# One transformer kernel: other stated orders at the beginning, in the feed-forward tails, around the attention block and in the PEER queries

## The chip, the cores and the metric

The kernel runs on one core of a Trainium2 chip. A core has five engines that each take their instructions in order: TensorE (PE) for matmuls, VectorE (DVE), ScalarE (ACT) and GpSimd (POOL) for elementwise work, and SyncE (SP), which issues most DMAs. The metric is device microseconds of one execution, the median of three runs.

## The reference

The input is a sequence of 256 tokens of width 1024 in float32, in two chunks of 128 tokens (chunk 0 and chunk 1). Two blocks follow each other. Cut to what matters:

```
h = h + 0.5 * swiglu(rms_norm(h, ln_ffn1), w1_gate, w1_up, w1_down)     # feed-forward 1
h = h + concat(hgrn2(...), latent_attention(...)) @ w_out               # mixer
h = h + 0.5 * swiglu(rms_norm(h, ln_ffn2), w2_gate, w2_up, w2_down)     # feed-forward 2
h = h + sigmoid(rms_norm(h, ln_ple) @ w_ple_gate) * (p @ w_ple_proj)    # per-layer gate
x = rms_norm(h, ln_final)

h1 = rms_norm(x, norm1) * (1 + sc1) + sh1                               # second block
y  = g_a * pool_mixer(h1) + g_b * forgetting_attention(q, k, v, log_f)  # 16 heads of 64
x  = x + gt1 * (y @ w_out)
h2 = rms_norm(x, norm2) * (1 + sc2) + sh2
q  = (h2 @ w_query)            # 8 heads x 2 halves x 128 = 16 query tiles of 128
sc = q . sub_keys -> top 16 of 128, twice -> top 16 of 256 candidates, softmax
x  = x + gt2 * sum over the chosen experts of gelu(h2 . expert_u) * gate * expert_v
out = rms_norm(x, final)
```

## The kernel before

Every matmul of two float32 operands is done as three products of parts: each operand is split into a high part (rounded, written by ACT, L289) and a low part (the rest, written by DVE, L290), and PE adds low x high, high x high and high x low (L319 to L321 with the tokens' tile as the stationary operand, L323 to L325 with the weights as the stationary one). Weights stream from memory in tiles of 128x1024: SP issues the DMA into `raw`, ACT and DVE split it into `wh` and `wl`, PE uses it.

The order of the work is the order of the program, changed by stated rules: `tc.issue_after(i)` puts what is written inside it behind instruction `i`, `behind_split(c)` behind the last high and low part of a normed chunk, `lag` says how many weight steps chunk 1 follows behind chunk 0, and small tables (FLAG, TLW, QORD, OUTS, YS) say which piece of work follows which. Tags and bank kinds ("mm", "sc", "pt", "acc") decide which buffer a tile gets and therefore what it waits for.

The places around the change:

- The beginning. `xload` (L268) brings `x` in four pieces on SP's queue; ACT's queue brings `col` (L272: small column constants) and two weights `w1t` in halves (L698). ACT's first activation needs `col`. The first projection works through eight weight steps for chunk 0 and, FLAG steps later, for chunk 1.
- The tails of the two feed-forward parts. The down projections of the last few tiles are put off to the end, where chunk 0 and chunk 1 each go through the pending weights; `aH`, `aL` are the parts of the last activations.
- The per-layer gate and the v projection. `ple` ends with a norm: sums of squares (L1176 to L1186), a power of -1/2 on POOL (L1196, L1199), `xs`, the scaled chunk (L458), and the scaling of the residual `xr` (L1201). `Norm.quad` (L467 to L481) transposes `xs` on PE, modulates it with `modc` on ACT and DVE, half of the columns each, into one tile `mod`, and splits that into `hH` and `hL`. The v projection (`wv`) then multiplies chunk 0 and chunk 1 with eight weights.
- The end of attention. The last heads' values, `y_tile` (L1380 to L1385, the sum of the two branches, transposed and split into `yH`, `yL`), the output projection `out_step`, `ev_out` (L1390, L1391: `gt`, and the new `xr`), the second norm (`ns` L420, `nv` L430, `ny` L431, `xs`), and the weights `qw` of the first four query tiles, which are split like all others.
- The PEER queries. `query(nt)` makes 24 matmuls with a streamed weight for nt of 4 and up and only two transposes for nt below 4, whose product has already been made in the attention block. `scores()` multiplies the query before last named with its keys (L1565) after ACT has copied it (`qT`, L1557).

## Time and profile before

| | us |
|---|---|
| median of three runs (lowest, highest) | 1575.57 (1574.95, 1575.89) |
| the profiled execution | 1574.45 |
| its span, first to last instruction | 1572.6 |
| PE busy | 1549.9 (99%) |
| DVE busy | 1125.7 (72%) |
| ACT busy | 806.6 (51%) |
| POOL busy | 83.0 (5%) |

Durations and stretches below come from the profiled execution. An engine counts as busy while it computes, not while it issues DMAs or waits on a semaphore. PE's matmuls overlap each other in its pipeline, so the time that one costs is the distance from its start to the next start, not its own duration. The idle time in brackets behind a row lies just before that instruction, on its engine; after `<-` stands what ended it.

### The profile page before, as it was taken

To read this page: it belongs to the slowest core of one execution; us is meant where nothing else is said; L and a number is where in the kernel's file an instruction comes from. 1 tells how busy PE (TensorE), PEld (TensorE's weight loads), DVE (VectorE), ACT (ScalarE), POOL (GpSimd) and SP (SyncE) were. 2 spreads that over 40 slices of the span, in tenths; PEclk is the share of its full clock that TensorE was granted. 3 is DMA by queue.
4 is the path that set the end of the run, shared out by engine and by line. 5 is a ranking of instruction groups with operands and counts; after the bars stand their busy time and mean duration, and the time that the engine had idled before them with its cause. 6 is when DMAs were issued, how large, how long until landed. Compare 5 with 4: busy or idle time off the path is not lost.

```text
span 1572.6 us, 27124 instructions
## 1 busy us (share of the span) xinstructions
PE 1549.9 (99%) x10317; PEld 1403.6 (89%) x10317; DVE 1125.7 (72%) x2206; ACT 806.6 (51%) x1533; POOL 83.0 (5%) x147
## 2 busy tenths in 40 slices
PE   9999999999999999999999999999999999999997
PEld 7999999879999879998899999999999877888886
DVE  7767768768866666557799988788986666555654
ACT  6444564554455656655554555544445445554543
POOL 1300011100000112011000000000000000000001
PEclk9999999999999999999999999999999999999999
DMA  8777754438976356442455655555446777666662
GB/s 315 242 259 255 246 170 135 140 104 298 337 227 228 123 189 200 134 135 94 150 162 186 187 175 165 162 158 161 161 158 199 248 227 232 191 190 195 215 189 87
DMA packets 84995, 299.94 MB, mean 191 GB/s; under 512 B 9632, under 2 KB 11264, under 8 KB 84608
## 3 DMA queue, kind: packets, MB, share of 16 engines
q1 hardware_dynamic: 80640, 290.86, 56.6%
q10 hardware_dynamic: 4224, 7.34, 1.4%
q8 instruction: 81, 1.33, 0.3%
q14 instruction: 50, 0.41, 0.1%
HBM read 294.95 MB, written 3.15 MB: 190 GB/s over the span
## 4 chain that ended last, share of the span: by engine, by line
PE 89%; DMA 4%; DVE 3%; ACT 2%; issue 1%; POOL 0%; ACTq 0%; POOLq 0%; DVEq 0%
PE mm L323 15%; PE mm L324 15%; PE mm L325 15%; PE acc L319 12%; PE acc L321 11%; PE acc L320 11%; DMA raw<-in_pv 2%; DMA raw<-in_wmod 2%; DVE wl L290 1%; PE acc L1673 1%; ACT wh L289 1%; PE acc L1674 1%; PE acc L925 1%; PE sc L1290 1%; PE mm L1565 0%
## 5 line engine op out<-in xcount | busy, mean ns | idle before, releaser
L289 ACT ACTIVATE wh<-raw 128x1024 fp32r<-128x1024 f32 (+3 forms) x605 | 528.3, 896 | 539.1 <-PE mm L324 251.9
L290 DVE TENSOR_TENSOR wl<-raw,wh 128x1024 fp32r<-128x1024 f32 (+3 forms) x605 | 611.2, 1027 | 264.7 <-ACT wh L289 260.0
L323 PE MATMUL mm<-hL,wh 128*128 128x256 f32 x1976 | 565.4, 286 | 0.0
L325 PE MATMUL mm<-hH,wl 128*128 128x256 f32 x1976 | 560.2, 284 | 0.0
L324 PE MATMUL mm<-hH,wh 128*128 128x256 f32 x1976 | 560.0, 283 | 0.0
L323 PEld LDWEIGHTS mm<-hL,wh 128*128 128x128 f32 x1976 | 377.6, 191 | 2.7
L324 PEld LDWEIGHTS mm<-hH,wh 128*128 128x128 f32 x1976 | 377.9, 191 | 2.0
L325 PEld LDWEIGHTS mm<-hH,wl 128*128 128x128 f32 x1976 | 377.4, 191 | 0.5
L319 PE MATMUL acc<-wh,aL 128*128 128x512 f32 x648 | 255.9, 395 | 1.6 <-DVE aL L290 1.6
L320 PE MATMUL acc<-wh,aH 128*128 128x512 f32 x648 | 253.0, 390 | 0.0
L321 PE MATMUL acc<-wl,aH 128*128 128x512 f32 x648 | 252.9, 392 | 0.0
L321 PEld LDWEIGHTS acc<-wl,aH 128*128 128x128 f32 x648 | 121.7, 188 | 28.2 <-issue 0.2
L319 PEld LDWEIGHTS acc<-wh,aL 128*128 128x128 f32 x648 | 121.9, 188 | 27.4 <-DVE aL L290 2.8
L320 PEld LDWEIGHTS acc<-wh,aH 128*128 128x128 f32 x648 | 121.8, 188 | 26.2 <-issue 0.5
L319 PE MATMUL acc<-wh,hL 128*128 128x512 f32 x224 | 89.3, 401 | 3.1 <-ACT wh L289 1.7
L320 PE MATMUL acc<-wh,hH 128*128 128x512 f32 x224 | 87.4, 392 | 0.0
L321 PE MATMUL acc<-wl,hH 128*128 128x512 f32 (+1 forms) x224 | 85.8, 391 | 0.0
L624 DVE SCALAR_TENSOR_TENSOR macc<-raw,col,macc 128x1024 f32<-128x1024 f32 x28 | 36.1, 1288 | 29.4 <-DMA raw<-in_wmod 29.3
L290 DVE TENSOR_TENSOR aL<-G,aH 128x256 fp32r<-128x256 f32 x128 | 53.6, 419 | 3.4 <-ACT aH L289 3.4
L319 PEld LDWEIGHTS acc<-wh,hL 128*128 128x128 f32 x224 | 42.5, 190 | 13.0 <-ACT wh L289 3.2
L289 ACT ACTIVATE aH<-G 128x256 fp32r<-128x256 f32 x128 | 51.2, 401 | 4.0 <-PE acc L321 4.0
L587 ACT ACTIVATE sg<-sg 128x256 f32<-128x256 f32 x36 | 14.8, 411 | 71.0 <-DVE sg L586 68.1
(469 smaller groups left out, 1620.9 us busy)
## 6 DMA issues: line engine op xcount, KB each, us to landing
raw<-in_pu SPq DMA_DIRECT2D x128, 512.0 KB, 3.5
raw<-in_pv SPq DMA_DIRECT2D x128, 512.0 KB, 4.3
raw<-in_wmod SPq DMA_DIRECT2D x48, 512.0 KB, 4.8
raw<-in_w1gu SPq DMA_DIRECT2D x36, 512.0 KB, 4.4
raw<-in_w2gu SPq DMA_DIRECT2D x36, 512.0 KB, 4.9
raw<-in_w1d SPq DMA_DIRECT2D x22, 512.0 KB, 4.8
raw<-in_w2d SPq DMA_DIRECT2D x22, 512.0 KB, 4.5
raw<-in_wout SPq DMA_DIRECT2D x16, 512.0 KB, 3.6
```

Source lines behind the costliest of these rows:

```text
L289: lasts["high"] = act.activation(H, src, AF.Copy)
L290: lasts["low"] = dve.tensor_sub(L, src, H.bitcast(F32))
L319: mm_(ps, aL, bH, start=start, stop=False)
L320: mm_(ps, aH, bH, start=False, stop=False)
L321: lasts["pe"] = mm_(ps, aH, bL, start=False, stop=stop)
L323: mm_(ps, aH, bL, start=start, stop=False)
L324: mm_(ps, aH, bH, start=False, stop=False)
L325: mm_(ps, aL, bH, start=False, stop=stop)
L624: dve.scalar_tensor_tensor(macc[j], raw, K("c", k), macc[j], op0=OP.mult, op1=OP.add)
L925: mm_(ps[:, j, c], k[pr][:, j, sl], q[pr][:, j, sl], start=True, stop=True)
L1290: mm_(ps[:, o:o + n], qa[:, hd, c * 128:c * 128 + 128], ka[:, hd, 0:n], start=True, stop=False)
L1673: mm_(ps[:, j], H[:, j], O[:, j], start=True, stop=False)
```

## The change

At the beginning `x` is loaded in pieces of other sizes, the two halves of the first weight come on ACT's queue ahead of `col`, the second weight's halves move to SP's queue, and chunk 1 follows two steps behind chunk 0 instead of four. In both tails the splits of the third and later weights stand behind the last `aH` and `aL`. In `Norm.quad` the tile `mod` is divided into two (one written by ACT, one by DVE), and the splits are made in pieces of 128x2x128. In `ple` the scaling of the residual moves from DVE to ACT, with a factor of its own (`q2`) from three small steps on POOL, and comes after chunk 1's split; the v weights get new places behind the squares, the sums, the split and the gates. At the end of attention the value bank of head 15 is of another kind, the loads of two pool weights stand behind the split, the low halves of three query weights go to GpSimd (POOL), and `ev_out(1, 1)` stands behind the low part of chunk 0. QORD, the order of the first PEER queries, interleaves the cheap and the full ones. The diff, cut to its core:

```diff
-FLAG = (4, 4)
+FLAG = (2, 4)
+TLA = (2, 2)
-QORD = [4, 5, 0, 1, 2, 3]
+QORD = [4, 0, 5, 1, 6, 2, 7, 3]
...
-    xload(0, 0)
+    xload(0, 0, 128)
     nc.sync.dma_start(cst[:, 0:128], A["cst"][:, 0:128])
-    nc.scalar.dma_start(col, A["col"])
+    xload(0, 128, 512)
...
     wraw1(0, 2, nc.scalar)
-    wraw1(1, 2, nc.scalar)
-    xload(1, 0)
+    nc.scalar.dma_start(col, A["col"])
+    wraw1(1, 2)
+    xload(1, 0, 512)
     wraw1(2)
-    xload(0, 1)
     wraw1(3)
-    xload(1, 1)
+    xload(0, 512, 1024)
+    xload(1, 512, 1024)
...
         def quads(self, c):
             for q in range(2):
                 self.quad(c, q)
+            for k in list(self.late) if c else ():
+                with self.behind_split(1), tc.high_priority(offset=-300):
+                    self.late.pop(k)()
...
-            m = self.mp.tile([128, 4, 128], F32, tag="mod", name="mod", bufs=2)
-            for i in range(4):
-                dt = 4 * q + i
-                if i < 2:
-                    act.activation(m[:, i], bk[:, i], AF.Identity, scale=self.gain(dt), bias=self.shift(dt))
-                else:
-                    dve.tensor_scalar(m[:, i], bk[:, i], self.gain(dt), self.shift(dt), op0=OP.mult, op1=OP.add)
-            self.last_hH[c] = act.activation(self.hH[:, qs, sl], m, AF.Copy)
-            self.last_hL[c] = dve.tensor_sub(self.hL[:, qs, sl], m, self.hH[:, qs, sl].bitcast(F32))
+            for u in range(2):
+                m = self.mp.tile([128, 2, 128], F32, tag="mod%d" % u, name="mod", bufs=2)
+                for i in range(2):
+                    dt = 4 * q + 2 * u + i
...
+                us = slice(4 * q + 2 * u, 4 * q + 2 * u + 2)
+                self.last_hH[c] = act.activation(self.hH[:, us, sl], m, AF.Copy)
+                self.last_hL[c] = dve.tensor_sub(self.hL[:, us, sl], m, self.hH[:, us, sl].bitcast(F32))
...
-            W = [wload(wd[f_], 1024, pw if n_ >= len(pend) - TLW[i - 1] else None) for n_, (f_, _) in enumerate(pend)]
+            W = []
+            for n_, (f_, _) in enumerate(pend):
+                with ExitStack() as order_:
+                    if n_ >= TLA[i - 1]:
+                        for a_ in last_a:
+                            order_.enter_context(tc.issue_after(ins_of(a_)))
+                    W.append(wload(wd[f_], 1024, pw if n_ >= len(pend) - TLW[i - 1] else None))
...
-                pool.tensor_scalar(v[:, 1:2], ss[:, 0:1], ss[:, 1:2], D * EPS, op0=OP.add, op1=OP.add)
-                pool.tensor_tensor(v[:, 1:2], v[:, 1:2], mhalf[:, 0:1], op=OP.pow)
-                with tc.high_priority(offset=-300), tc.issue_after(ins_of(nout.last_xs[c])):
-                    dve.tensor_scalar(xr[:, c], hg[c], v[:, 1:2], 32.0, op0=OP.mult, op1=OP.mult)
+                def late():
+                    pool.tensor_scalar(u, ss[:, 0:1], ss[:, 1:2], D * EPS, op0=OP.add, op1=OP.add)
+                    pool.tensor_tensor(u, u, mhalf[:, 0:1], op=OP.pow)
+                    pool.tensor_scalar(u, u, 32.0, None, op0=OP.mult)
+                    act.activation(xr[:, c], hg[c], AF.Copy, scale=u)
...
         def wv(kt):
-            with tc.issue_after(ins_of(nin.last_xs[0])) if kt < 5 else nin.behind_split(0):
+            with ExitStack() as order_:
+                if kt > 0:
+                    order_.enter_context(tc.issue_after(ins_of(nin.squares[0])))
+                    order_.enter_context(tc.issue_after(ins_of(nin.sums[0] if kt < 2 else nin.last_xs[0])))
+                if kt > 1:
+                    order_.enter_context(nin.behind_split(0))
+                if kt > 2:
+                    order_.enter_context(tc.issue_after(ins_of(nin.gates[1])))
                 return wload(A["wv"][kt])
...
-            po = bank("mm" if hd >= POM else "pt", (128, 2, 64))
+            po = bank("sc" if hd == 15 else "mm" if hd >= POM else "pt", (128, 2, 64))
...
-                split(raw[:, sl], H[:, sl], L[:, sl])
+                if i == 0:
+                    split(raw[:, sl], H[:, sl], L[:, sl])
+                else:
+                    act.activation(H[:, sl], raw[:, sl], AF.Copy)
+                    pool.tensor_sub(L[:, sl], raw[:, sl], H[:, sl].bitcast(F32))
...
-        with tc.issue_after(ins_of(pT_read)), tc.issue_after(ins_of(ysum)):
+        with tc.issue_after(ins_of(pT_read)):
             query_w(1)
-        with tc.issue_after(ins_of(yhigh)), tc.issue_after(ins_of(ysum)):
+        with tc.issue_after(ins_of(yhigh)):
             query_w(2)
             query_w(3)
-        ev_out(1, 1, acc[1, 1])
+        with tc.issue_after(ins_of(nout.last_hL[0])):
+            ev_out(1, 1, acc[1, 1])
```

How this moves instructions is shown at three places, engine by engine; a row is the line, the operation, what it writes and reads, and the shape. First ACT at the beginning of the program, before:

```order
L272 DMA col<-in_col 128x120
L698 DMA raw<-in_w1t 128x512 x4
L510 ACT_TABLE_LOAD
L510 ACTIVATE hH<-mm,col 128x128
L289 ACTIVATE wh<-raw 128x512 x2
L510 ACTIVATE hH<-mm,col 128x128
L289 ACTIVATE wh<-raw 128x512
L510 ACTIVATE hH<-mm,col 128x128 x2
```

and after:

```order
L713 DMA raw<-in_w1t 128x512 x2
L716 DMA col<-in_col 128x120
L518 ACT_TABLE_LOAD
L518 ACTIVATE hH<-mm,col 128x128
L290 ACTIVATE wh<-raw 128x512 x3
L518 ACTIVATE hH<-mm,col 128x128
L290 ACTIVATE wh<-raw 128x512
L518 ACTIVATE hH<-mm,col 128x128
```

`col` stood first on ACT's queue and stands third now, behind the halves of the first weight; four halves (two weights) are two.

Second GpSimd (POOL) at the end of attention, where `ns` and `ny` are small steps of the second norm (8227, 8244 and the powers 8253, 8270 for chunk 0, the others for chunk 1) and `qw11`, `qw21`, `qw31` the low parts of three query weights; before:

```order
L1351 TENSOR_TENSOR ga_6230<-ga_6230,y_8007 128x256
L420 TENSOR_SCALAR ns_8227<-ns_8227 128x1
L431 TENSOR_TENSOR ny_8253<-nv_8252,mhalf_92 128x1
L420 TENSOR_SCALAR ns_8274<-ns_8274 128x1
L431 TENSOR_TENSOR ny_8377<-nv_8376,mhalf_92 128x1
L311 CAST wh_8507<-hL_6222 128x1
```

and after:

```order
L1382 TENSOR_TENSOR ga_6233<-ga_6233,y_8024 128x256
L1497 TENSOR_TENSOR qw11_8358<-raw_8359,qw10_8357 128x512 x2
L1497 TENSOR_TENSOR qw21_8366<-raw_8367,qw20_8365 128x512 x2
L1497 TENSOR_TENSOR qw31_8374<-raw_8375,qw30_8373 128x512 x2
L421 TENSOR_SCALAR ns_8244<-ns_8244 128x1
L421 TENSOR_SCALAR ns_8291<-ns_8291 128x1
L432 TENSOR_TENSOR ny_8270<-nv_8269,mhalf_92 128x1
L432 TENSOR_TENSOR ny_8400<-nv_8399,mhalf_92 128x1
L312 CAST wh_8536<-hL_6225 128x1
```

Six low halves now stand ahead of the norm's steps, and chunk 0's power (`ny`) stands behind chunk 1's `ns`.

Third ACT at the first PEER queries, where `wh` is the high part of a streamed query weight, `qT` the copy of a query and `G` that of its scores; before:

```order
L289 ACTIVATE wh_8699<-raw_8697 128x1024
L1557 ACTIVATE qT_8536<-mm_8504 128x256
L289 ACTIVATE wh_8750<-raw_8748 128x1024
L1557 ACTIVATE qT_8570<-mm_8538 128x256
L1567 ACTIVATE G_8478<-mm_8572 128x256
L1557 ACTIVATE qT_8593<-mm_8590 128x256
L1567 ACTIVATE G_8478<-mm_8595 128x256
L1557 ACTIVATE qT_8609<-mm_8606 128x256
L1567 ACTIVATE G_8478<-mm_8611 128x256
```

and after:

```order
L290 ACTIVATE wh_8715<-raw_8713 128x1024
L1593 ACTIVATE qT_8565<-mm_8533 128x256
L1593 ACTIVATE qT_8570<-mm_8567 128x256
L1603 ACTIVATE G_8507<-mm_8572 128x256
L290 ACTIVATE wh_8779<-raw_8777 128x1024
L1593 ACTIVATE qT_8622<-mm_8590 128x256
L1603 ACTIVATE G_8507<-mm_8624 128x256
L1593 ACTIVATE qT_8638<-mm_8635 128x256
L1603 ACTIVATE G_8507<-mm_8640 128x256
L290 ACTIVATE wh_8823<-raw_8821 128x1024
L1593 ACTIVATE qT_8683<-mm_8651 128x256
```

Before, two weight splits come with the first two copies and then none until the transposed queries are through; now a split precedes every second copy.

## Rows read from the trace of the kernel before

**Rows 1.** what PE waited for over the whole run: us in total, times, longest

```profile
PE acc L319 <- DVE hL L481: 4.3, 3, 1.7
```

**Rows 2.** windows: length, then busy us of PE, PEld, DVE, ACT, POOL; PEclk; DMA

```profile
5.00:16.00 11.00, 9.61 (x46) 6.59 (x45) 7.14 (x13) 7.89 (x16) 0.49 (x1) 1.00 1.03 397
505.00:530.00 25.00, 25.00 (x126) 20.86 (x125) 16.10 (x31) 13.00 (x30) 0.92 (x3) 1.00 0.73 246
550.00:560.00 10.00, 8.02 (x37) 6.43 (x36) 9.88 (x22) 4.82 (x11) 0.20 (x1) 0.83 0.57 211
560.00:570.00 10.00, 8.61 (x42) 6.61 (x41) 6.54 (x15) 4.37 (x13) 3.78 (x6) 1.00 0.26 79
725.00:765.00 40.00, 35.00 (x181) 28.18 (x181) 28.26 (x63) 21.67 (x50) 2.35 (x7) 1.00 0.39 139
765.00:800.00 35.00, 34.37 (x290) 34.02 (x290) 30.42 (x144) 17.68 (x35) 0.00 (x0) 1.00 0.46 145
```

**Rows 3.** timeline of ACT, beginning: start, us, instruction, [idle before <-releaser]

```profile
4.33 1.28 ACT L510 ACT_TABLE_LOAD   x1 [4.33 <-DVE col L715]
...
7.49 0.63 ACT L289 ACTIVATE wh<-raw 128x512 fp32r<-128x512 f32 x1 [0.65 <-DMA raw<-in_w1t]
```

**Rows 4.** timeline of PE, beginning

```profile
6.89 0.50 PE L319 MATMUL acc<-wh,hL 128*128 128x512 f32 x1 [0.17 <-ACT wh L289]
...
16.02 0.48 PE L319 MATMUL acc<-wh,hL 128*128 128x512 f32 x1
```

**Rows 5.** DMA issues of the beginning: count, KB each, median us to landing

```profile
col<-in_col ACTq DMA_DIRECT2D x1, 60.0 KB, 3.3
```

**Rows 6.** timeline of DVE, between norm and modulation of block 2

```profile
547.03 4.90 DVE L290 TENSOR_TENSOR wl<-raw,wh 128x512 fp32r<-128x512 f32 x8
...
553.71 0.16 DVE L644 TENSOR_TENSOR modc<-fill,col 128x8 f32<-128x8 f32 x1
```

**Rows 7.** timeline of PE, v projection, chunk 1

```profile
564.72 1.09 PE L472 MATMUL mm<-cst,xs 128*128 128x128 f32 x8
...
568.49 0.50 PE L319 MATMUL acc<-wh,hL 128*128 128x512 f32 x1 [1.28 <-DVE hL L481]
```

**Rows 8.** timeline of DVE, end of attention

```profile
737.22 2.49 DVE L290 TENSOR_TENSOR qw<-raw,qw 128x512 fp32r<-128x512 f32 x4
...
739.63 1.29 DVE L1390 TENSOR_TENSOR gt<-acc,gt 128x512 f32<-128x512 f32 x2
...
744.53 0.89 DVE L458 TENSOR_SCALAR xs<-xr,ny 128x512 f32<-128x512 f32 x2 [0.69 <-POOL ny L431]
```

**Rows 9.** timeline of PE, starts of the two chunks' queries

```profile
749.30 0.50 PE L319 MATMUL acc<-qw,hL 128*128 128x512 f32 x1 [1.71 <-DVE hL L481]
...
757.36 0.51 PE L319 MATMUL acc<-qw,hL 128*128 128x512 f32 x1 [1.35 <-DVE hL L481]
```

**Rows 10.** GpSimd: lines L1351, L1820 (ns min/median/max) and its timeline

```profile
L1351 POOL TENSOR_TENSOR ga<-ga,y x8: 736/739/1118, 608.9 to 718.6; 128x256 f32<-128x256 f32 x8
...
L1820 POOL TENSOR_TENSOR G<-G x2: 1297/1301/1305, 1558.3 to 1560.8; 128x512 f32<-128x512 f32 x2
...
49.91 1.70 POOL L664 TENSOR_SCALAR n<-n 128x256 f32<-128x256 f32 x1
```

**Rows 11.** timelines of ACT (two rows) and PE, first PEER queries

```profile
768.87 1.06 ACT L289 ACTIVATE wh<-raw 128x1024 fp32r<-128x1024 f32 x1 [1.31 <-PE mm L324]
...
769.84 0.36 ACT L1557 ACTIVATE qT<-mm 128x256 f32<-128x256 f32 x1
...
769.24 0.38 PE L1553 MATMUL mm<-cst,G 128*128 128x128 f32 x2
...
770.25 0.71 PE L1565 MATMUL mm<-keys,qT 128*128 128x128 f32 x4 [0.64 <-ACT qT L1557]
...
770.80 0.38 PE L1553 MATMUL mm<-cst,G 128*128 128x128 f32 x2
...
771.02 0.61 PE L1565 MATMUL mm<-keys,qT 128*128 128x128 f32 x4
```

More of the change, by code (lines that the diff above doesn't have):

```diff
@@ L266, in _build, with xload @@
     xv = A["x"].rearrange("(c p) d -> p c d", p=128)
-    def xload(c, j):
-        nc.sync.dma_start(xr[:, c, j * 512:j * 512 + 512], xv[:, c, j * 512:j * 512 + 512])
-    xload(0, 0)
+    def xload(c, a, b):
+        nc.sync.dma_start(xr[:, c, a:b], xv[:, c, a:b])
+    xload(0, 0, 128)
     nc.sync.dma_start(cst[:, 0:128], A["cst"][:, 0:128])
-    nc.scalar.dma_start(col, A["col"])
+    xload(0, 128, 512)
     def C(name, a=0, n=None):
@@ L444, in __init__ @@
             self.s, self.xs, self.last_xs, self.mp = {}, {}, {}, nxp
-            self.last_hH, self.last_hL = {}, {}
+            self.last_hH, self.last_hL, self.late = {}, {}, {}
         def part(self, c, j):
@@ L592, in ffn @@
                 split(a, aH, aL)
+                last_a = lasts["high"], lasts["low"]
                 pend.append((f, (aH, aL)))
@@ L1157, in ple @@
             st, hg = {}, {}
+            squares, sums = nout.squares, nout.sums = {}, {}
+            nout.gates = {}
             gf = p1.tile([128, D], F32, name="gf")
@@ L1166, in ev @@
                 with nout.behind_split(0) if c else nullcontext():
-                    act.activation(t, ps, AF.Tanh, scale=nin.half[c])
+                    nout.gates[c] = act.activation(t, ps, AF.Tanh, scale=nin.half[c])
                     dve.scalar_tensor_tensor(t, t, 1.0, proj[:, c, sl], op0=OP.add, op1=OP.mult)
@@ L1184, in ev @@
                 else:
-                    act.activation(sq[:, 0:256], g[:, 0:256], AF.Square, accum_out=ss[:, 3:4])
+                    squares[c] = act.activation(sq[:, 0:256], g[:, 0:256], AF.Square, accum_out=ss[:, 3:4])
                     dve.scalar_tensor_tensor(sq[:, 256:], g[:, 256:], 1.0, g[:, 256:], op0=OP.mult, op1=OP.mult,
@@ L1193, in after @@
                 ss = st[c]
-                v = nrm.tile([128, 2], F32, tag="q1", name="q1")
-                dve.tensor_scalar(v[:, 0:1], ss[:, 3:4], ss[:, 4:5], ss[:, 5:6], op0=OP.add, op1=OP.add)
+                v = nrm.tile([128, 1], F32, tag="q1", name="q1")
+                sums[c] = dve.tensor_scalar(v[:, 0:1], ss[:, 3:4], ss[:, 4:5], ss[:, 5:6], op0=OP.add, op1=OP.add)
                 pool.tensor_tensor(v[:, 0:1], v[:, 0:1], mhalf[:, 0:1], op=OP.pow)
                 nout.chunk(c, hg[c], v[:, 0:1])
-                pool.tensor_scalar(v[:, 1:2], ss[:, 0:1], ss[:, 1:2], D * EPS, op0=OP.add, op1=OP.add)
-                pool.tensor_tensor(v[:, 1:2], v[:, 1:2], mhalf[:, 0:1], op=OP.pow)
-                with tc.high_priority(offset=-300), tc.issue_after(ins_of(nout.last_xs[c])):
-                    dve.tensor_scalar(xr[:, c], hg[c], v[:, 1:2], 32.0, op0=OP.mult, op1=OP.mult)
+                u = nrm.tile([128, 1], F32, tag="q2", name="q2")
+                def late():
[3 more added lines that the diff above has]
+                    act.activation(xr[:, c], hg[c], AF.Copy, scale=u)
+                nout.late[c] = late
             wl_ = [lambda k=k: wload(A["wpg"][k], 1024, pw if k >= 8 - PLW else None) for k in range(8)]
@@ L1325, in pool_group @@
             wp = sm.tile([128, 256], F32, tag="wp", name="wp")
-            nc.scalar.dma_start(wp, A["wpool"][:, g * 256:(g + 1) * 256])
+            with nin.behind_split(1) if g < 2 else nullcontext():
+                nc.scalar.dma_start(wp, A["wpool"][:, g * 256:(g + 1) * 256])
             psc = sm.tile([128, 256], F32, tag="psc", name="psc")
```

8 lines of the change are left out of this document (7 added, 1 removed).

## The prediction

> **What bounds the kernel now.** The page's engine table (shown above with the times) comes first: the reader sees there that PE is busy 99% of the span, so a step pays only where PE stands idle. The list of PE's waits comes next. Its largest entry is the wait for `hL` of a norm (L481, 4.3 us over three waits) [rows 1]. Then I set windows around each place that the change touches, and the reader compares PE's busy time with the length of each window [rows 2]. Idle time is 11.00 - 9.61 = 1.39 us at the beginning, nothing in 505 to 530 (the second feed-forward tail; the first looks the same), 1.98 + 1.39 = 3.37 us in 550 to 570 (the v projection), 5.00 us in 725 to 765 (the end of attention), and 0.63 us in 765 to 800 (the PEER queries). So no more than about 10.4 us can be won in all, and a PE delay at 775 goes through to the end, for PE has next to no idle time behind it that could swallow one. Timelines of single engines in those windows give the terms below.
>
> **The beginning.** Before, `col` is the first transfer on ACT's queue. ACT's table load waits 4.33 us for the scaled `col`; the second half of the first weight then waits 0.65 us for its DMA and comes only at 7.49 [rows 3]. PE's first matmul is at 6.89, and chunk 1 starts at 16.02 [rows 4]. After, `col` (60 KB, 3.3 us from issue to landing [rows 5]) stands behind two transfers of 256 KB. What these 512 KB cost I bound from both sides: if the queue never filled, `col` would be later by its later issue alone, about 1 us, and land at about 5; if it waited for both, it would land where the second half weight now lands, about 7.4 [rows 3]. I take 5.3, nearer to the first, because the many small pieces of `col` no longer go ahead of the large ones. The table load, the first high half and the first matmul are then about 0.7 us later (7.6). But the weights of the first two steps are there by that time, and with chunk 1 only two steps behind (FLAG 2) PE has more to do. If then no wait for weights is left, 1.39 us of idle time go and 0.7 is paid by the later start; with 0.1 for stalls of single matmuls that go too, that is a gain of 0.8 us. Ends: a gain of 1.6 (all of it, `col` in time) and a loss of 0.4 (`col` at 7.4; the start is then 2.7 later, against which stand at most 2.3 us of waits for weights and for chunk 1's turn).
>
> **The v projection.** Before, DVE does eight `wl` halves (4.90 us), the scaling of the residual and two more halves between `xs` and `modc` at 553.71 [rows 6]. PE waits for that, and the mean granted clock of 550 to 560 is 0.83 [rows 2]: after those idle microseconds and matmuls of one column it falls from its upper level (2.4 GHz) to the lower (1.2) for a while. After, `modc`, the modulation and `hL` follow `xs` at once, so chunk 0's projection starts some 2.3 us earlier. It doesn't end earlier: chunk 1's transposes start at 564.72 [rows 7] because its own norm ends there, and that chain is hardly shorter. ACT issues four DMAs back to back and splits three weights before the squares of chunk 1, and on GpSimd two small steps for the new `q2` stand ahead of the power that `xs` needs. So PE's idle time moves from 552-554 to about 561-564.7. What is won lies behind it: with `hL` in pieces of 128x256 instead of 128x512, PE can start chunk 1 after the first piece, about 567.8 instead of 568.49 [rows 7]: 0.7 us. If the idle microseconds there bring the lower clock, as those before did, transposes and two weight steps at half the pace eat it: -0.1. I take a gain of 0.3, between the two. Ends: 1.8 gain (chunk 1's norm earlier by most of chunk 0's 2.3) and 0.8 loss (its chain late by one more weight).
>
> **The end of attention.** Before, four low halves of query weights (2.49 us on DVE) stand between the last `yL` and `gt` at 739.63; `xs` follows at 744.53 [rows 8]. PE starts chunk 0's queries at 749.30 after 1.71 us of waiting and chunk 1's at 757.36 after 1.35 [rows 9]. After, six low halves are on GpSimd. DVE now has `yL` of tile 7 behind four weight halves and waits for `yL` of tile 6 first, so the outputs of chunk 0 end 0.7 us later on PE; `gt` can still start at about 738.9. `xs` needs the power step on GpSimd, which stands behind the low halves and behind the sum of chunk 1's squares; PE has only the 24 output matmuls of chunk 1 to fill the time. A low half (two inputs, 128x512) has near rows: 1.30 us for the same shape and form (L1820), 0.74 us in the median and 1.12 at most for 256 columns (L1351); the dearest is 1.70 for 256 columns, at 49.91 [rows 10]. So the bounds are 1.30 and 3.4 us (twice 1.70), and I take 1.6, near the row of the same shape and stretched a little for a busy DVE. The last four halves start once ACT has their first high half, about 736.7; they end at 743.1, before the sum of chunk 1's squares (about 743.8), which the power must follow anyway. The power then ends at about 744.6, as now, and `xs` is at most 0.2 later. The smaller pieces shorten the way from transposes to the first `hL` by a good microsecond, so chunk 0 starts at about 748.3 (1.0 earlier) and chunk 1, whose output follows `hL` at once, at about 755.9 (1.4 earlier, which takes the first in). I take 1.4. Ends: 3.0 gain (three fifths of the 5.00 idle) and 4.5 loss (rival 2). Each low half over 1.6 us shifts the chain by four times the excess.
>
> The Trainium skill, GPSIMD Engine Reference, section 1 (Specifications), says that GpSimd's way into SBUF is shared with VectorE and contends with VectorE instructions that read two SBUF inputs, as `wl` and `xr` do. The longest and the median of L1351, 1.118 / 0.739 = 1.5 [rows 10], fit that. An estimate by it would be 1.30 x 1.5 = 1.95 us for a low half and the chain 1.4 us later; by it the gain of this part is gone and the time 1577.1 us, inside the likeliest case's own range.
>
> **The queries.** The order 4,5,0,1,2,3 becomes 4,0,5,1,6,2,7,3. Queries 4 and up are 24 matmuls with a streamed weight; 0 to 3 are two transposes. The scores of a query come one query later. Before, only query 5's scores follow their own 24 matmuls with little between. The rows show what that costs: ACT first splits the next weight, whose buffer those matmuls just freed (768.87, 1.06 us), then copies `qT` (769.84, 0.36). PE starts its two transposes at 769.24; such a pair takes 0.22 (770.80 to 771.02), so from 769.46 to 770.25 it does nothing: 0.79 us [rows 11]. After, four queries (4 to 7) have only transposes and a cheap query's scores between their matmuls and their own scores, and in ACT's order the weight split stands ahead of `qT` each time. Queries 5, 6 and 7 cost 0.79 each; query 4 has no cheap scores before it, which take about 0.45 (770.25 to 770.80 less the start-up): 1.24. Together 3.6 us; gone are the 0.79 and some 0.2 of small gaps between the cheap ones. Cost: 2.6 us, all of it on PE. Ends: 0 (ACT gets `qT` out first) and 3.6.
>
> **Feed-forward tails.** The window is full [rows 2], so there is nothing to gain: 0. The splits of the third and later tail weights now wait behind the last `aH`/`aL`; PE meanwhile works on the first two weights of both chunks. If that cover were too short, one split (1.06 us on ACT, as in [rows 11]) would show. Ends: 0 and a loss of 1.1.
>
> **Sum.** -0.8 - 0.3 - 1.4 + 2.6 + 0 = +0.1 us. The profiled execution took 1574.45 us (span 1572.6 and 1.85 around it); the median of the runs, 1575.57, stands 1.12 above it. 1574.45 + 0.1 + 1.12 gives 1575.7 us. What a measurement can tell from no change is about 0.2%, or 3.15 us.
>
> **Rivals.** (1) Faster: the query order costs nothing, because `qT` leaves ACT before the weight split is due, and the end of attention gives its upper 3.0: -0.8 - 0.3 - 3.0 + 0 = -4.1, so 1571.5 us. For it: ACT is busy only 17.68 of 35 us in 765 to 800 [rows 2]. Against: where it matters the rows have the split first, then `qT` [rows 11]. (2) Slower: GpSimd's queue decides. At 3.4 us for a low half, four of them end at 750.3, and the power of chunk 0's norm, with it `xs`, the transposes and `hL`, comes 5.8 us later than now. PE can fill some of it with output matmuls that it now does earlier; chunk 0's queries start at about 754, 4.5 us late. Sum: -0.8 - 0.3 + 4.5 + 2.6 = +6.0, so 1581.6 us. It eats into the gain from 1.6 us per half on and makes the whole slower by 0.2% from about 2.7. For it: 1.70 us at 49.91; against: 1.30 for the very form [rows 10]. (3) The beginning loses: `col` lands at 7.4, +0.4 instead of -0.8, 1576.9 us. (4) In the v projection the change does nothing but move the idle time, and the lower clock with it: +0.1 instead of -0.3, 1576.1 us.
>
> **Chances.** My forecast with (3) and (4), within 0.2%: 0.54. Rival (1), and other sums of upper ends that pass 3.15 us: 0.25 faster. Rival (2), and sums of lower ends: 0.21 slower. The range from 1571.0 to 1579.5 takes in rival (1) and a low half of up to about 2.7 us; of (2) the dear end is left out. The likeliest case by itself lies between 1573.3 and 1577.6.
>
> **What would show it.** In the profile after: the table load before 5.8 us and chunk 1's first matmul before 15.5; the v projection's first matmul near 553.7, a wait of PE near 561 to 564.7, chunk 1 near 567.8; low halves on POOL of 1.3 to 1.6 us, with `ny` right behind a sum of squares and not behind a low half; four waits of PE for `qT` of 0.8 to 1.2 us between query matmuls. Wrong would be: no such waits (rival 1), POOL halves above 2.5 us with `ny` behind them (rival 2), or a gap that opens in a tail.

## The result, and the profile after

| kernel | median | lowest to highest (executions) | ratio to before, 95% interval | profiled span |
|---|---|---|---|---|
| before | 1575.57 us | 1574.06 to 1575.89 (5) | | 1572.6 us |
| changed | 1584.98 us | 1581.58 to 1586.58 (5) | 1.006 [1.0046, 1.0073] | 1584.7 us |

The change is slower by 9.4 us; the forecast was 1575.7, in a range up to 1579.5. The profiled execution of the changed kernel (1586.58) is 12.1 us longer than that of before; it is the slowest of its five, so the stretches below add up to more than 9.4. I compare the starts of TensorE's matmuls, number by number ("matmul 200" is the 200th), in the two traces; where the difference grows, time is lost:

| stretch | forecast | measured in the profiled pair |
|---|---|---|
| beginning (to matmul 200, 40 us) | -0.8 | +3.3 |
| both feed-forwards, steadily (the second with its tail) | none | +0.6 and +0.9 |
| first feed-forward tail, with the block behind it | 0 | +1.7 |
| v projection | -0.3 | 0.0 |
| end of attention (to chunk 1's queries) | -1.4 | +1.7 |
| queries | +2.6 | +3.0 |
| last stage (waits at 1293 and 1317) | none | +1.2 |

The list of PE's waits in the changed kernel (total, count, longest in us) answers to [rows 1]:

```profile
PE mm L476 <- DVE xs L459: 3.7, 1, 3.7
PE acc L320 <- ACT wh L290: 3.4, 3, 1.6
PE mm L1601 <- ACT qT L1593: 3.0, 4, 1.1
PE acc L320 <- DVE yL L1416: 2.4, 1, 2.4
...
PE acc L320 <- DVE hL L489: 1.8, 2, 0.9
PE mm L514 <- DMA xr<-in_x: 1.1, 1, 1.1
```

The wait for `hL`, largest before, fell from 4.3 to 1.8 us; those for `xs`, `wh`, `qT`, `yL` and x are new or longer. The windows of the same places (columns as in [rows 2], shifted by the delay up to there) give the sizes:

```profile
5.00:16.00 11.00, 8.27 (x30) 6.40 (x29) 6.47 (x12) 6.87 (x12) 0.96 (x1) 0.69 1.01 392
511.00:536.00 25.00, 25.00 (x124) 20.30 (x123) 20.45 (x36) 14.84 (x31) 0.00 (x0) 1.00 0.83 279
556.00:566.00 10.00, 10.00 (x54) 8.55 (x53) 9.53 (x22) 9.15 (x23) 0.77 (x1) 1.00 0.33 107
566.00:576.00 10.00, 6.32 (x26) 5.01 (x25) 6.12 (x17) 4.97 (x14) 4.08 (x6) 0.83 0.32 109
731.00:771.00 40.00, 35.26 (x168) 27.47 (x168) 27.09 (x63) 21.07 (x52) 10.23 (x13) 0.96 0.35 123
771.00:806.00 35.00, 32.01 (x264) 31.01 (x263) 29.97 (x145) 16.29 (x33) 0.00 (x0) 1.00 0.45 145
```

**Beginning.** PE is busy 8.27 of 11 us, before 9.61 [rows 2], and at a mean clock of 0.69. Timelines of PE and ACT, then two DMA issues (count, KB each, us to landing), against [rows 3 to 5]:

```profile
6.29 0.55 PE L514 MATMUL mm<-cst,xr 128*128 128x128 f32 x3 [1.15 <-DMA xr<-in_x]
...
8.96 0.80 PE L320 MATMUL acc<-wh,hL 128*128 128x512 f32 x1 [1.58 <-ACT wh L290]
9.55 0.63 PE L321 MATMUL acc<-wh,hH 128*128 128x512 f32 x1
9.98 0.63 PE L320 MATMUL acc<-wh,hL 128*128 128x512 f32 x1
...
6.73 1.28 ACT L518 ACT_TABLE_LOAD   x1 [6.73 <-DVE col L731]
8.02 0.37 ACT L518 ACTIVATE hH<-mm,col 128x128 fp32r<-128x128 f32 x1
...
xr<-in_x SPq DMA_DIRECT2D x1, 192.0 KB, 4.6
...
col<-in_col ACTq DMA_DIRECT2D x1, 60.0 KB, 4.8
```

Two transfers are late: x's second piece lets the transposes go on only at 6.29, `col` lets the table load start only at 6.73. The table load comes last of the two: it ends at 8.01, and the first high half (`hH`) begins at 8.02. The first projection matmul starts at 8.96, 2.07 later than before; the waits that go behind it give back 1.4 (e4 below starts as late, and is 0.6 behind at matmul 100). Then the matmuls stand 0.43 us apart instead of 0.23: the granted clock is at its lower level (1.2 GHz) up to 15.1 us, and that is the larger loss, about 2 us. The rest, 0.6, is a wait at 35 us.

**Queries.** Four waits, as forecast; the first, then one of the three that are alike:

```profile
775.48 0.71 PE L1601 MATMUL mm<-keys,qT 128*128 128x128 f32 x4 [1.08 <-ACT qT L1593]
...
780.36 0.71 PE L1601 MATMUL mm<-keys,qT 128*128 128x128 f32 x4 [0.64 <-ACT qT L1593]
...
774.10 1.06 ACT L290 ACTIVATE wh<-raw 128x1024 fp32r<-128x1024 f32 x1 [1.66 <-PE mm L325]
775.06 0.64 ACT L1593 ACTIVATE qT<-mm 128x256 f32<-128x256 f32 x2
```

ACT splits the next weight (774.10) and only then copies `qT` (775.06), the order of [rows 11]. Measured from start to start against the usual spacing of such matmuls, the waits are 1.24 and three times 0.80 us, 3.64 in all against 3.6 in the forecast. Only 0.6 of the 1.0 us that I took off again is gone, so the stretch costs 3.0.

**v projection.** Chunk 0 starts at 560.34 and chunk 1's transposes at 571.07 after 3.68 us of waiting, 6.6 and 6.4 us behind the forecast places (553.7 and 564.7), as everything is by then. Idle time has moved (3.68 us from 556 to 576; before 3.37 from 550 to 570), and the lower clock with it (0.57 from 571 to 575).

**End of attention.** GpSimd, DVE and PE, against [rows 8, 9]:

```profile
743.32 5.57 POOL L1497 TENSOR_TENSOR qw<-raw,qw 128x512 fp32r<-128x512 f32 x4 [4.10 <-ACT qw L1496]
...
753.19 0.57 POOL L432 TENSOR_TENSOR ny<-nv,mhalf 128x1 f32<-128x1 f32 x1
...
740.47 0.42 DVE L1416 TENSOR_TENSOR yL<-mm,yH 128x256 fp32r<-128x256 f32 x1 [2.97 <-ACT yH L1415]
...
741.66 3.57 DVE L291 TENSOR_TENSOR wl<-raw,wh 128x512 fp32r<-128x512 f32 x4
745.15 0.41 DVE L1416 TENSOR_TENSOR yL<-mm,yH 128x256 fp32r<-128x256 f32 x1
...
748.03 1.40 DVE L1422 TENSOR_TENSOR xr<-gt,xr 128x512 f32<-128x512 f32 x1
...
745.62 0.80 PE L320 MATMUL acc<-wh,yL 128*128 128x512 f32 x1 [2.40 <-DVE yL L1416]
746.21 0.63 PE L321 MATMUL acc<-wh,yH 128*128 128x512 f32 x1
```

The power `ny` stands 4.3 us behind the end of the last low half: GpSimd's queue doesn't decide. Late is `yL` of tile 7, behind that of tile 6 and four splits. One of the splits took 1.76 us instead of 0.69, and one `xr` 1.40, both beside low halves: each ended 0.55 us after the low half that was running when it began (ends at 744.68 and 748.88). PE waits 2.40 us and then runs eight matmuls at the lower clock, most of them 0.63 us long, which costs 1.7 us more (745.62 to 749.34 for nine spacings of 0.23).

The wait doesn't always bring the lower clock. e6, e10 and e16 below have the same code here; PE waits as long in them, and the clock stays up. PE of e16:

```profile
740.87 0.50 PE L320 MATMUL acc<-wh,yL 128*128 128x512 f32 x1 [2.38 <-DVE yL L1416]
741.21 0.40 PE L321 MATMUL acc<-wh,yH 128*128 128x512 f32 x1
```

In these three traces the end of attention is 0.2 us longer than before, in the changed kernel's 1.7; 1.5 of that is the clock.

### The profile page after: what moved, and what is told of

Read it like the earlier page. It is cut to its first block, busy times and chain, and to the rows that moved or that the text cites. A ratio compares the mean times of both kernels' runs of the same rounds, so it can differ in the third digit from the quotient of the medians.

```text
span 1584.7 us, 27141 instructions
## 1 busy us (share of the span) xinstructions
PE 1556.2 (98%) x10317; PEld 1405.7 (89%) x10317; DVE 1123.7 (71%) x2206; ACT 809.4 (51%) x1545; POOL 95.5 (6%) x155
## 4 chain that ended last, share of the span: by engine, by line
PE 84%; DMA 7%; DVE 4%; ACT 3%; issue 2%; POOL 0%; ACTq 0%; POOLq 0%; DVEq 0%
PE mm L324 14%; PE mm L325 14%; PE mm L326 14%; PE acc L320 11%; PE acc L322 11%; PE acc L321 11%; DMA raw<-in_wmod 3%; DVE wl L291 2%; DMA raw<-in_pv 2%; ACT wh L290 1%; PE acc L1709 1%; PE acc L1710 1%; PE acc L941 1%; PE sc L1320 1%; PE mm L1601 1%
## 5 line engine op out<-in xcount | busy, mean ns | idle before, releaser
L320 PE MATMUL acc<-wh,hL 128*128 128x512 f32 (+1 forms) x224 | 89.6, 403 | 1.8 <-ACT wh L290 1.8
L321 PE MATMUL acc<-wh,hH 128*128 128x512 f32 (+1 forms) x224 | 88.2, 396 | 0.0
```

What stands on the lines that cost most here:

```text
L320: mm_(ps, aL, bH, start=start, stop=False)
L321: mm_(ps, aH, bH, start=False, stop=False)
```

## Experiments

Times are medians with the ratio to before on the same chip. A "wait" is PE's start-to-start excess over the usual spacing. Single executions of one kernel with the new beginning lie 3 to 8 us apart (e4: 1580.47 to 1588.50), so each reading rests on a median together with a trace.

**The beginning.** e1: the old transfers and lag.

```
-FLAG = (2, 4)                      +FLAG = (4, 4)
-xload(0, 0, 128) ... xload(0, 128, 512)
+xload(0, 0) ... nc.scalar.dma_start(col, A["col"])
-wraw1(1, 2)                        +wraw1(1, 2, nc.scalar)
...
```

> The changed kernel with the old beginning (the order and pieces of the first transfers, and FLAG 4). Theory 'col': in the trace after, col lands at 6.44 instead of 4.04 us, the first projection matmul starts at 8.96 instead of 6.89, and PE's clock is at its lower level from 8.28 to 15.10; by the 200th matmul that is 3.25 us behind. So about 3.2 us come back: some 1581.8 us, 6.2 above the kernel before, matmul 200 again near 40.1 us and no low clock before 16 us. Rival 'elsewhere': the beginning only shifts work, and what is lost by 40 us returns later in the first feed-forward: within 1 us of 1585.

1581.10 us, 1.0031 [1.002, 1.0042]: 3.9 us less than the changed kernel. Matmul 200 starts 3.0 earlier, as 'col' said (3.2), and the wait in the first tail is gone too. Is it `col`? e6 puts only that back:

```
 xload(0, 128, 512)
+nc.scalar.dma_start(col, A["col"])
 wraw1(0, 2, nc.scalar)
-nc.scalar.dma_start(col, A["col"])
```

> The changed kernel with one transfer put back: the columns of constants (60 KB) are issued on ACT's queue ahead of the first weights, as before; x stays cut at 128 columns, the second weight tile stays on SP's queue, and the first projection's lag stays 2. Theory 'col': col lands near 4.0 us instead of 6.44, the table load and the first hH follow at 4.4 and 5.7 as before, and the first projection matmul starts at about 7 instead of 8.96; matmul 200 starts near 41 instead of 43.4, the time falls by 2 to 3 us to about 1582.5. Rival 'the other transfers': x or the weights land late because of what goes ahead of them on SP's queue; the first projection matmul still starts past 8.5, and the time stays at 1584 to 1585.

1583.03 us, 1.0046 [1.0031, 1.0061]. PE and ACT of that run:

```profile
7.03 0.90 PE L515 MATMUL mm<-cst,xr 128*128 128x128 f32 x3 [1.75 <-DMA xr<-in_x]
...
8.90 0.80 PE L321 MATMUL acc<-wh,hL 128*128 128x512 f32 x1
...
3.27 1.28 ACT L519 ACT_TABLE_LOAD   x1 [3.27 <-DVE col L731]
7.96 0.37 ACT L519 ACTIVATE hH<-mm,col 128x128 fp32r<-128x128 f32 x1 [3.41 <-PE mm L515]
```

The table load is early (3.27), yet the first matmul starts at 8.90 as in the changed kernel: it now waits for x's second piece (7.03). The rival holds for the start. e10 puts `col` and an uncut x first:

```
-xload(0, 0, 128)                   +xload(0, 0, 512)
-xload(0, 128, 512)                 +nc.scalar.dma_start(col, A["col"])
...
```

> The changed kernel with x's first 512 columns in one transfer again, issued first, and col first on ACT's queue; the second weight tile stays on SP's queue, the order of the rest of x and the lag of 2 stay. With col alone put back, x's second piece landed at 7.03 us and the first projection matmul stayed at 8.90. Theory 'x and col, either of which is late': now the transposes run at 4.9 us, the first hH is done before 6.5, the first projection matmul starts at about 7, TensorE keeps its upper clock, matmul 200 starts near 40.5 and the time falls by 3 us to about 1582. Rival 'the weight on SP's queue': the second weight tile is late behind x, PE waits for it after the first step, and matmul 200 starts past 41.5.

1581.51 us, 1.0037 [1.0025, 1.0049]. PE:

```profile
6.68 0.50 PE L320 MATMUL acc<-wh,hL 128*128 128x512 f32 x1 [0.68 <-ACT wh L290]
```

The first matmul starts at 6.68, the clock stays at 1.00, and matmul 100 is 0.6 us ahead of before. So x's second piece alone can hold the start (e6), and with both transfers early it is gone; `col` late alone was not run. But PE waits 5.15 us in the first tail (below) in this profiled execution, the slowest of six. e16 changes the lag alone:

```
-FLAG = (2, 4)
+FLAG = (4, 4)
```

> The changed kernel with chunk 1's first projection again four steps behind chunk 0's (FLAG 4 in place of 2); all transfers as in the changed kernel. Theory 'transfers': x's second piece and col still land past 6 us, the first projection starts near 8.9, matmul 200 at 41 to 43.5; the weight stream stays 2 to 4 us further behind than PE at the 56th weight; the time is that of the changed kernel, 1585. Rival 'lag': the four steps let weights be used up as they come, the stream's lead is back (under 1.5 us lost at the 56th weight), the first tail has no wait, and the time falls to about 1582.5.

1582.11 us, 1.0046 [1.0033, 1.006], as the rival 'lag' has it: the first matmul still starts late (8.54), but the clock stays up in this trace, the weight stream is not behind any more and the first tail has no wait.

**The first tail.** e3 takes the rule for the tail's weights out:

```
-TLA = (2, 2)
+TLA = (99, 99)
```

> The changed kernel without the rule that the splits of the third and later tail weights stand behind the last aH and aL, in both tails. Theory 'tail': PE's wait of 1.75 us at 192.69 goes, since the tail weights are split before the last activation again; 1.6 us come back, some 1583.4 us, and PE is busy through 185 to 200. Rival 'mixer weights': the wait comes from the weights of the mixer that stand in the same queue, and it stays or moves to the second tail: less than 0.5 us.

1585.46 us, 1.0054 [1.004, 1.0067]; the wait stays (1.66 us from start to start). The rule isn't its cause. In the changed kernel and in e10 it is, on PE:

```profile
194.67 0.50 PE L320 MATMUL acc<-wh,aL 128*128 128x512 f32 x1 [1.59 <-ACT wh L290]
```

```profile
194.72 0.79 PE L320 MATMUL acc<-wh,aL 128*128 128x512 f32 x1 [4.99 <-ACT wh L290]
```

PE waits for weights that ACT has not split yet. e13 and e14 go on from there: before with the rule, and e10 without it.

```
e13: before, +TLA = (2, 2)
e14: as e10, -TLA = (2, 2)  +TLA = (99, 99)
```

> The kernel before with one part of the change: in both feed-forward tails the splits of the third and later down weights wait for the last aH and aL. Theory 'lead': this order costs only where the weight stream reaches the tail late; with the old beginning it arrives early, PE does not wait at 190, and the time stays within 0.5 us of before, 1575 to 1576. Rival 'order by itself': the four weights hold their load buffers until the last a, the mixer's weights come late behind them, and PE waits 1 to 2 us at about 190; 1576.5 to 1577.5.

1577.03 us, 1.0014 [1.0005, 1.0023]. No wait in the first tail; PE is even 0.6 us earlier behind it. But two more splits then stand between `xs` and `modc` in the old v projection's order. DVE, then PE:

```profile
548.72 6.10 DVE L291 TENSOR_TENSOR wl<-raw,wh 128x512 fp32r<-128x512 f32 x10
...
557.70 0.50 PE L320 MATMUL acc<-wh,hL 128*128 128x512 f32 x1 [3.99 <-DVE hL L482]
```

Ten `wl` halves where [rows 6] has eight, and PE waits 2.15 us longer than in the wait of 1.84 that before has there. Neither theory had that place; the rival's time (1576.5 to 1577.5) came out for another reason.

> The changed kernel with x and col early again (as in the run before it, where PE then waited 5.15 us in the first tail) and without the rule for the tail's weights. Theory 'lead and order together': with the weights split as soon as they land, the wait in the first tail falls under 1.7 us, and the time by about 2 us to 1579.5. Rival 'lead alone': the stream is late in any order, the wait in the tail stays above 3 us, and the time at 1581.5.

1583.37 us, 1.0056 [1.0042, 1.007]: the wait in the tail is gone in its trace, but the median is above e10's. Inconclusive, because its weight stream was not late in that execution. What goes with the wait is this: by how much the 57th weight split on ACT (153.0 us in before) came later than before, less PE's own delay there, against the wait in the first tail:

| kernel | e16 | e13 | e14 | e1 | e2 | e7 | e3 | e9 | e6 | changed | e4 | e10 |
|---|---|---|---|---|---|---|---|---|---|---|---|---|
| stream behind PE, us | -2.5 | -2.0 | 1.3 | 1.4 | 1.4 | 2.1 | 2.7 | 2.8 | 3.4 | 3.8 | 3.8 | 5.5 |
| wait in the tail, us | 0 | 0 | 0 | 0 | 0 | 0.8 | 1.7 | 0.6 | 2.0 | 1.8 | 2.1 | 5.1 |

So the wait goes with a weight stream that has lost its lead since the beginning. It opens from about 2 us on, and its size differs from one execution to the next. The lag decides more than the transfers: in the nine traces with the lag of 2 the stream is 1.3 to 5.5 us behind, and seven of them have the wait; in the eight with the lag of 4 it is between 2.7 ahead and 1.8 behind, and none has it.

**The place in SBUF.** The changed kernel and the first four experiments all show the steady loss in the feed-forwards. e5 is before, with a tile made wider and no instruction changed:

```
-v = nrm.tile([128, 2], F32, tag="q1", name="q1")
+v = nrm.tile([128, 16], F32, tag="q1", name="q1")
```

> The kernel before with one number changed: the two small scaling tiles are 64 bytes wide instead of 8, so that every tile that stands behind them in SBUF lies 64 bytes further, as in the changed kernel; no instruction is added, removed or moved. In the changed kernel, and in all four experiments so far, the down matmuls of both feed-forwards (512 columns, the a halves as weights) stand 233 ns apart in place of 227 ns, about 0.55 us in each of the two stages. Theory 'place in SBUF': the spacing is 233 ns here too, and the span grows by 1.1 us, to about 1573.7, the time to about 1576.7. Rival 'order': the spacing comes from the neighbours in time, so it stays at 227 ns and the time at 1575.6.

1577.33 us, 1.0011 [1.0002, 1.002]. PE of before, of e5, the same down matmuls:

```profile
72.19 0.39 PE L319 MATMUL acc<-wh,tL 128*128 128x512 f32 x1
72.42 0.39 PE L320 MATMUL acc<-wh,tH 128*128 128x512 f32 x1
72.64 0.39 PE L321 MATMUL acc<-wl,tH 128*128 128x512 f32 x1
72.87 0.39 PE L319 MATMUL acc<-wh,tL 128*128 128x512 f32 x1
73.10 0.39 PE L320 MATMUL acc<-wh,tH 128*128 128x512 f32 x1
```

```profile
72.28 0.40 PE L319 MATMUL acc<-wh,tL 128*128 128x512 f32 x1
72.52 0.39 PE L320 MATMUL acc<-wh,tH 128*128 128x512 f32 x1
72.75 0.40 PE L321 MATMUL acc<-wl,tH 128*128 128x512 f32 x1
72.98 0.39 PE L319 MATMUL acc<-wh,tL 128*128 128x512 f32 x1
73.21 0.40 PE L320 MATMUL acc<-wh,tH 128*128 128x512 f32 x1
```

Five starts span 0.91 us before and 0.93 here. Over the 490 or so spacings of this kind in the two feed-forwards the mean goes from 229 to 234 ns. 'Place in SBUF' holds: 64 bytes that a new small tile (`q2`) takes shift the tiles behind it. The size came out above my 1.1: in e5's trace PE loses 1.05 us in each feed-forward, tail included, 2.1 in all, as in the median. Of the 1.7 us that the table above gives to the first tail, some 0.4 are of this kind.

**The queries.** e2:

```
-QORD = [4, 0, 5, 1, 6, 2, 7, 3]
+QORD = [4, 5, 0, 1, 2, 3]
```

> The changed kernel with the old order of the PEER queries. Theory 'lag of one': the four waits of PE for qT (1.24, 0.80, 0.80, 0.80 us) become one of 0.8; 2.6 us come back, some 1582.4 us. Rival 'hidden': the sorting on DVE after the queries sets the pace, and the waits only stand in its place: less than 0.7 us come back.

1579.84 us, 1.0027 [1.0018, 1.0036]. One of the four waits is left (0.80), and PE is 3.0 us earlier behind them; that trace has no waits in the first tail and at 1293 either, which the order of the queries doesn't reach, so the rest of the 5.1 us that its median is lower can't be put down to the order. The term holds.

**The end of attention.** e4: low halves back on DVE.

```
-if i == 0: split(...)
-else: act.activation(H...); pool.tensor_sub(L...)
+split(raw[:, sl], H[:, sl], L[:, sl])
```

> The changed kernel with the low halves of the three query weights on DVE again; all other orders at the end of attention as in the changed kernel. Theory 'shared way': beside GpSimd's low halves two DVE operations with two inputs took 1.76 (wl at 743.47) and 1.40 us (xr at 748.03) instead of 0.69; with the halves on DVE these are 0.69 again, and 1.5 to 2 us come back (1583.3). Rival 'order': what holds DVE is that yL of tile 7 stands behind yL of tile 6 and four weight halves; with six low halves more on DVE (0.60 each) nothing comes back or up to 2 us are added (1585 to 1587), and PE's wait before the output matmuls of tile 7 (2.56 us at 742.83) is as long or longer.

1580.92 us, 1.004 [1.0025, 1.0056]. DVE, then PE:

```profile
738.90 2.49 DVE L291 TENSOR_TENSOR wl<-raw,wh 128x512 fp32r<-128x512 f32 x4
...
741.78 0.50 PE L320 MATMUL acc<-wh,yL 128*128 128x512 f32 x1 [1.30 <-DVE yL L1416]
742.12 0.39 PE L321 MATMUL acc<-wh,yH 128*128 128x512 f32 x1
```

The four splits take 2.49 instead of 3.57 us, PE's wait is 1.1 shorter, and a 0.78 wait for `xs` shows instead. The clock doesn't fall, so the end of attention is 2.0 us shorter and no longer than before. But against e6, e10 and e16, where the clock doesn't fall either and the low halves are on GpSimd, it is only 0.5 us shorter: that much of the 2.0 is shown to be the low halves' price, and the 1.5 to 2 us of 'shared way' is not. The Trainium skill, GPSIMD Engine Reference, section 1 (Specifications), has GpSimd's way into SBUF shared with VectorE. The trace agrees, but the price fell on the two-input work of DVE (0.69 to 1.76 us) and less on the low half (1.30, at most 1.73 here and 1.83 in e9).

Why is there a wait at all? e7 puts two waits for `ysum` back as well:

```
as e4, and
+with ..., tc.issue_after(ins_of(ysum)): query_w(1)
+with ..., tc.issue_after(ins_of(ysum)): query_w(2) ...
```

> The changed kernel with two parts of the attention block's end put back: the queries' low halves on VectorE, and the second and third query weights held until ysum. With the low halves alone put back, PE still waited 1.47 us for yL of tile 7 and 0.78 us for xs. Theory 'VectorE's order': the weights' splits that were let ahead of yL cost that wait; without them it falls under 0.8 us, and with the smaller pieces of the last Norm the attention end is then about 1 us shorter than before, the time about 1580. Rival 'ysum was no brake': the wait stays at 1.4 to 1.5 us and the time at 1580.9, that of the low halves alone.

1584.35 us, 1.0059 [1.0046, 1.0072]; the wait is 2.69, longer. My theory falls: the low halves that e4 lets go early fill DVE while it waits for tile 6; held for `ysum` they stand ahead of `yL` of tile 7. e9 tries the bank:

```
-po = bank("sc" if hd == 15 else "mm" if hd >= POM else "pt", (128, 2, 64))
+po = bank("mm" if hd >= POM else "pt", (128, 2, 64))
```

> The changed kernel with one part put back: head 15's products go into a bank of kind mm again, not sc. In the changed kernel TensorE's order has the transposes of tile 6 only behind five steps of the output projection, 2.25 us ahead of those of tile 7 (before: 5.65 us), and PE waits 2.56 us for yL of tile 7. Theory 'bank': with the old bank the transposes of tile 6 are back between heads 14 and 15, and the wait for yL of tile 7 falls to 0.7 to 1.0 us; the time falls by 1.6 us, to about 1583.4. Rival 'low halves': the wait comes from VectorE's two-input instructions, one stretched to 1.76 us by GpSimd's low halves; it stays above 2 us, and the time at 1585.

1584.57 us, 1.0059 [1.0046, 1.0072]. PE:

```profile
750.98 1.11 PE L476 MATMUL mm<-cst,xs 128*128 128x128 f32 x8 [1.82 <-DVE xs L459]
```

The wait for `yL` is gone, and PE waits 1.82 for `xs` instead. The end of attention is 2.2 us shorter in the trace; the clock stays up there, and against e6, e10 and e16 it is 0.7 shorter. The median shows none of it, which the spread of that kernel's five runs (1581.07 to 1586.71) can hide. So e15 does the bank alone, on before. TensorE's order then differs in one thing:

```
-MATMUL mm<-cst,gb 128x128 x2
-MATMUL mm<-v_6229,pT 128x64   (six of head 15)
+MATMUL sc<-v_6229,pT 128x64   (the same six)
 ... five steps of the output projection
+MATMUL mm<-cst,gb 128x128 x2
```

> The kernel before with one part of the change: head 15's products in a bank of kind sc. This alone moves the transposes of tile 6 in TensorE's order from between heads 14 and 15 to behind five steps of the output projection. Theory 'bank': yL of tile 6 is then late on VectorE, the splits behind it too, and PE waits 2 to 2.7 us for yL of tile 7 (before 0.75); chunk 0's queries start some 1.5 to 2 us later, and the time is about 1577.2. Rival 'only with the rest': VectorE has cover for it, the wait stays under 1.2 us, the time at 1575.5.

1578.25 us, 1.0017 [1.0008, 1.0026]: slower by the bank alone. PE:

```profile
739.40 0.51 PE L319 MATMUL acc<-wh,yL 128*128 128x512 f32 x1 [2.52 <-DVE yL L1385]
```

The wait is 2.69 (before 0.75), and chunk 0's queries start 2.7 us later; 1.9 of that is the wait, and the clock falls here too (from 740.9 to 744.3). 'Bank' is shown for the wait, by taking the bank out (e9) and by putting it in (e15).

**What is worth keeping.** e8 keeps the v projection's order and the two-piece quads; e11 is before with the quads alone; e12 adds to e11 the freed query weights and the later last output.

```
e11: -m = ...tile([128, 4, 128]...)
     +for u in range(2): m = ...tile([128, 2, 128]...)
e12: as e11, -tc.issue_after(ins_of(ysum)) (twice)
     +with tc.issue_after(ins_of(nout.last_hL[0])): ev_out(1, 1, ...)
e8:  the changed kernel with all else put back, u in pool p
```

> The changed kernel with every part put back but the v projection's order and the smaller pieces of the Norm (two tiles of 128x2x128 in place of one of 128x4x128), and with the second scaling tile in a pool that opens later, so that the feed-forwards' tiles lie where they lay before. Theory: the beginning, the tails and the queries are as before, the down matmuls are 227 ns apart, the waits for the query weights' first tile are 1.0 and 1.1 us instead of 1.88 and 1.51, and the v projection comes out even: about 1.3 us faster than before, 1574.2. Rival 'the v projection loses': its early start is given back with up to 1 us more, and the time is that of before, 1575.5, or more.

> The kernel before with one part of the change: the Norm's quads in two pieces of 128x2x128 instead of one of 128x4x128. Theory: the first hL piece is ready sooner, so PE's waits ahead of chunk 0's and chunk 1's queries (1.88 and 1.51 us of excess) fall to about 1.6 and 1.1, and that ahead of chunk 1 in the v projection (1.45) falls by some 0.5; about 1.2 us faster, 1574.2. Rival: the twice as many small instructions on ACT and VectorE eat it; the waits stay, the time is 1575.3 or more.

> The kernel before with the two-piece quads and two further parts of the change: the second and third query weights no longer wait for ysum, and chunk 1's last output waits for the first hL of chunk 0. Theory: to the gain of the two-piece quads comes that chunk 1's output no longer stands between modulation and hL on VectorE, so PE's wait ahead of chunk 0's queries falls from about 1.6 to 1.0 us; 1573.5. Rival: the weights' splits that are let go earlier push yL of tile 7 back, PE waits 0.7 us more there, and the time is that of the two-piece quads alone or above it.

e8: 1574.02 us, 0.9997 [0.9989, 1.0006]; e11: 1574.77, 0.9997 [0.9988, 1.0005]; e12: 1575.51, 0.9997 [0.9988, 1.0006]. The quads do what was expected of them: waits ahead of the queries of 1.60 and 1.10 us or less in all three (1.88 and 1.51 before). But the gain of 0.7 us can't be told from no change, and in e12 PE waits 1.41 for `xs` (0.78 before), so that nothing is left. No version beats the kernel before beyond what can be measured. In e8 the feed-forwards run at the spacing of before again.

## Why the prediction was wrong

- **Beginning, -0.8: wrong, the first step that failed.** `col` landed at 6.44, inside my bounds of 5 and 7.4 but above the 5.3 I took. The table load came at 6.73 and not before 5.8. I had bounded `col` alone and never priced the cut of x, whose second piece landed at 6.24 as the third transfer of SP's queue; e6 shows that this alone can keep the start at 8.9. The start came 2.07 late, not 0.7; the waits that go gave back 1.4, as I had it. Above all I had no term for the clock here, though I had one in the v projection: e4 started at 8.91 with the same waits, its clock stayed up, and at matmul 200 it was 2.7 us ahead of the changed kernel (2.1 the clock, 0.6 the wait at 35 us). My bound of a loss of 0.4 counted a late start against waits that go, both at full clock.
- **Tails, 0: wrong.** A gap opened in a tail, the sign that I had named, and it is larger than my end of 1.1 us. I looked for cover in the tail itself. What goes with the wait is the lead that the weight stream has by then, and the new lag takes it away (e16 and the table). The rule for the tail's weights costs elsewhere (e13).
- **End of attention, -1.4: wrong in sign.** The gains that I named came: PE's waits ahead of the two queries' chunks fell to 1.00 and 1.08. I said that `yL` of tile 7 would come behind four splits, and put that at 0.7 us. The size failed: PE waits 2.56 (before 0.75), and in the profiled execution a lower clock follows. With the clock down the part comes out at +1.7, with the clock up at +0.2, and neither is near -1.4. I gave the bank of head 15 no term, though it moves the transposes of tile 6 (e15), and I bounded the low half's own length where the length of DVE's work beside it mattered (about 0.5 us, e4). My estimate of 1.95 us put the price on each low half; five of six took 1.29 to 1.37. Rival 2's time, 1581.6, is nearer than my forecast, but its mechanism isn't there.
- **Queries, +2.6: right** in the place and size of each wait (e2); the stretch cost 3.0, because I took 0.4 too much off for what goes.
- **v projection, -0.3: right in mechanism**; it came out as rival 4 has it, idle time moved and no more. Its order was run only together with the two-piece quads (e8).
- **Not in the sum at all:** the place in SBUF (about 2 us, e5). Together with the tail and the lower clock it makes more than half of the 12.3 us, and the sum had nothing for any of the three there.
- **Open:** the 1.2 us of the last stage. The waits at 1293 and 1317 differ from run to run, before has 1.54 and 0.43 at two such places in its profiled execution and e5 none over 0.35; and e14's median.

## What to carry over

A stated order has to be priced by all that it moves: a bank that frees one wait can move a transpose behind five steps and open a longer one. Where PE is busy 99% of the time, a wait costs its length and, in some executions, what the lower clock adds behind it; a prediction should carry both cases, and two traces should be compared at the same clock before a difference is put down to an edit. A delay at the start shows again where the weight stream was about to need its lead. A sum of small edits that nearly cancel (here +0.1) says little when single terms can miss by 3 or 4 us, and terms that share a stream or a clock don't add (e1, e2 and e4 each give back 3.9 to 5.1 us of a loss of 9.4).

## What was not expected of the hardware

- 64 bytes more in front of the feed-forwards' tiles made their 512-column matmuls 5 ns longer from start to start (mean 229 to 234), and with the old place it is gone (e8). Of the operands of these matmuls only the stationary ones (`tH`, `tL`, `aH`, `aL`) moved; the moving weights `wh` and `wl` kept their place. Whether it is the place of these or of other tiles that moved was not tried.
- The fall to the lower clock differs between executions of the same code: it fell in the changed kernel after waits of 1.15 and 1.58 us and not in e4 after 1.52 and 1.57; at the end of attention it fell in the changed kernel after 2.40 and not in e6, e10 and e16 after 2.38 to 2.39. In e6 the clock's column reads 1.00 where matmuls stand 0.43 apart, so the spacing is the better sign.
- A low half on GpSimd beside DVE cost DVE more (a split of 1.76 and an `xr` of 1.40 us instead of 0.69; in e9 two `xr` of 1.47 and 1.79) than itself (1.30 usually, 1.83 at most). Each of these four DVE instructions ended 0.54 or 0.55 us after the low half that was running when it began, as if it had waited for its end.
